# Low parts of the weight tiles: VectorE subtractions replaced by accumulating DMAs in SBUF, four weight buffers instead of three

## The chip, the cores and the metric

The kernel runs on one core of one Trainium2 chip. The metric is the device time of one execution in microseconds (us), as the median of several runs of the same kernel. Engines carry the names that the profile uses: PE is TensorE's matmuls and PEld its weight loads, DVE is VectorE, ACT is ScalarE, POOL is GpSimd, SP is SyncE, whose queue issues most DMAs.

## What is computed

Two identical layers of a hybrid decoder trunk over 512 positions and a model width of 1024, all inputs float32. Cut to what matters:

```python
h = rms_norm(x, ln_mix)
z = h @ w_in                                  # 1024 -> 6440 columns, split into the branches
o_nsa = nsa_attention(...)                    # compressed, selected and window attention, 8 heads
o_gla = gated_linear_attention(...)           # 4 heads, chunked
o_mem = memory_attention(...)                 # cross-attention into 256 memory tokens
merged = sum(gates[b] * (o_b @ w_branch[b]))  # three branches, 512 -> 1024 each
x = x + merged @ w_out
h = rms_norm(x, ln_mlp)
x = x + square(relu(h @ w_up)) @ w_down       # 1024 -> 4096 -> 1024
```

## The kernel before, in words

All large products are made in float32 quality from the faster `float32r` type. Each operand is split in two: a high part, which is the value rounded to `float32r`, and a low part, which is the value minus its high part. `mm3` (line 459) then makes three matmuls for one product: high by high, high by low and low by high. The activations are split once by `split` (line 492, high part on ACT, low part on DVE). The weights stream in: 128x1024 tiles of 512 KB, 298 whole ones and two more that come in halves at the start, 150 a layer.

`weights` (line 447) brings one tile in and takes three buffers from rings of three: `raw` for the loaded values, `wh` for the high part, `wl` for the low part. A load is issued on SP's queue, ACT casts `raw` to `wh`, and `self.low()` (line 360) names the engine that subtracts `wh` from `raw` into `wl`: DVE, except in the sparse-attention stage, where `share` is 4 and each fourth one goes to POOL. `raw` is free for the next load when both readers are done; `wh` and `wl` are free when the last matmul that reads them is done. `blockT` (line 604) uses a tile for 24 matmuls of 512 columns, `chunkM` (line 643) for 24 or 48 of 256 columns, `nsa_cmp` (line 1141) for 8 of 256 columns. `gate_proj` (line 841) takes one `raw` and one `wh` buffer from the same rings, for a small matrix whose two parts lie in one tile; it is made by ACT and DVE and stays so.

`layer` (line 1514) runs the stages of a layer: norm and compression keys, key and value projections, the compression MLP (`nsa_cmp`) woven with query and GLA projections, sparse attention woven with more projections, gated linear attention (GLA, `gla_attn`) woven with the first branch and the second gate, memory attention, the third branch, output projection, and the MLP, whose 64 tiles a layer serve 24 matmuls of 512 columns each.

The order of the instructions on each engine isn't the order of the code. `Order` (line 131) records every call with a cost from its table `time` (line 145), its tile dependencies and the rings' reuse, and `schedule` (line 234) lists the whole program on a time line of its own: `lat` gives the waiting time from one instruction to the next by the first one's engine. The order found is then forced on every engine's queue by dependencies. Since all calls go through one recording helper, nearly every instruction in the profile has line 312; rows are told apart by their tiles.

The names in the profile: `ps_d`, `ps_s`, `ps_t`, `ps_o` are PSUM banks; `xg` the split and scaled layer input, `u` the split hidden activations of the MLP or the merged branches; `nP`, `nd`, `nkraw`, `nqraw` belong to sparse attention; `ge`, `gke`, `gqz`, `gqe`, `gat`, `gS`, `grsa`, `grsy` to GLA; `xscr` is the scratch in HBM that carries `x` from the first layer to the second.

Of the kernel before, what the change touches and what calls it, by code (L numbers as in the profile page):

```python
# [9 lines left out]
F32 = mybir.dt.float32  # L10
F32R = mybir.dt.float32r
I32 = mybir.dt.int32
U8 = mybir.dt.uint8
AF = mybir.ActivationFunctionType
OP = mybir.AluOpType
# [4 lines left out]
P = 128  # L20
# [3 lines left out]
KT = D // P  # L24
# [106 lines left out]
class Order:  # L131
# [4 lines left out]
    def __init__(self, tc):  # L136
        self.tc = tc
        self.ins, self.eng, self.cost, self.pre = [], [], [], []
        self.load = []
        self.hist = {}  # L140
        self.first, self.ring, self.uses = {}, [], {}
        self.gone = []

    @staticmethod
    def time(eng, op, out, ins, accum):
# [27 lines left out]
    def note(self, eng, op, args, kw, r):  # L173
        is_ap = lambda x: hasattr(x, "tensor") and hasattr(x, "free_size")
        out = kw["out"] if "out" in kw else args[0]
        ins = [x for x in list(args[0 if "out" in kw else 1 :]) + [v for k, v in kw.items() if k not in ("out", "accum_out")] if is_ap(x)]
        outs = [out] + ([kw["accum_out"]] if "accum_out" in kw else [])
        k = len(self.ins)
        self.ins.append(r.ins)
        self.eng.append(eng)  # L180

        self.load.append(0.0 if eng != "tensor" else ins[0].free_size() / (2400 if op == "transpose" else 1200))
        self.cost.append(self.time(eng, op, out, ins, len(outs) > 1 and eng == "scalar"))
        pre = set()
        for w, aps in ((False, ins), (True, outs)):
            for x in aps:
                n = x.tensor.name
                h = self.hist.setdefault(n, [])
                if w and n in self.first:
                    f, prev, heads, m = self.first[n]  # L190
                    pre.update(f)
                    if prev:
                        self.ring.append((prev, k))
                    heads[m].append(k)
                    if m and heads[m - 1]:
                        pre.add(heads[m - 1][0])
                self.uses.setdefault(n, set()).add(k)
                a, b, c, d = g = self.region(x)
                keep = []
                for e in h:  # L200
                    (a2, b2, c2, d2), w2, k2 = e
                    if a < b2 and a2 < b and c < d2 and c2 < d:
                        if (w or w2 or x.space == PSUM) and k2 != k:
                            pre.add(k2)
                        if (w or x.space == PSUM) and k2 != k and a <= a2 and b2 <= b and c <= c2 and d2 <= d:
                            continue
                    keep.append(e)
                keep.append((g, w, k))
                self.hist[n] = keep
        self.pre.append(pre)  # L210
# [23 lines left out]
    def schedule(self):  # L234

        after = [[] for _ in self.pre]
        for k, p in enumerate(self.pre):
            for q in p:
                after[q].append(k)

        wait = {"sync": (2.0, 2.0), "tensor": (0.2, 0.0), "vector": (0.13, 0.25), "scalar": (0.14, 0.27), "gpsimd": (0.1, 0.1), "none": (0.0, 0.0)}

        def lat(a, b):
            return wait[self.eng[a]][self.eng[b] == "tensor"]


        start, end = self.go(self.pre, after, range(len(after)), lat, COLD)
        best = end, start
        for _ in range(3):
            back, end = self.go(after, self.pre, [-s - c for s, c in zip(start, self.cost)], lambda a, b: lat(b, a), 0.0)  # L250
            start, end = self.go(self.pre, after, [end - s - c for s, c in zip(back, self.cost)], lat, COLD)
            best = min(best, (end, start))
        self.start = best[1]
        info = mybir.DependencyInfo(mybir.DependencyClass.NoSync, mybir.DependencyReason.DATA)
        lines = {}
        for k in sorted(range(len(self.ins)), key=lambda k: self.start[k]):
            lines.setdefault(str(self.ins[k].engine), []).append(k)
        for o in lines.values():
            for a, b in zip(o, o[1:]):
                self.tc.add_manual_dep(self.ins[b], self.ins[a].name, info, reason="order")  # L260
# [91 lines left out]
class Builder:  # L352
# [93 lines left out]

    def weights(self, src, n=1024, parts=1):
        nc = self.nc
        raw = self.wp.tile([P, 1024], F32, name="raw", tag="raw", bufs=3)
        h = self.wp.tile([P, 1024], F32R, name="wh", tag="wh", bufs=3)  # L450
        l = self.wp.tile([P, 1024], F32R, name="wl", tag="wl", bufs=3)
        for p in range(parts):
            c = slice(p * n // parts, (p + 1) * n // parts)
            nc.sync.dma_start(raw[:, c], src[:, c])
            nc.scalar.copy(h[:, c], raw[:, c])
            self.low().tensor_sub(l[:, c], raw[:, c], h[:, c])
        return h, l

    def mm3(self, out, ops, start=True, stop=True):
# [381 lines left out]
    def gate_proj(self):  # L841

        nc = self.nc
        w = self.wp.tile([P, 1024], F32R, name="wh", tag="wh", bufs=3).rearrange("p (k x m) -> p k x m", k=KT, x=2)
        raw = self.wp.tile([P, 1024], F32, name="raw", tag="raw", bufs=3)[:, :512]
        nc.sync.dma_start(raw, self.a["ws"][self.l])
        r = raw.rearrange("p (k m) -> p k m", k=KT)
        nc.scalar.copy(w[:, :, 0], r)
        nc.vector.tensor_sub(w[:, :, 1], r, w[:, :, 0])
        ps = self.pd()  # L850

        for x, (h, l) in enumerate(self.xs()):
            both = w[:, x].rearrange("p x m -> p (x m)")
            self.nc.tensor.matmul(ps, both, h, start=x == 0, stop=False)
            self.nc.tensor.matmul(ps, both, l, start=False, stop=x == KT - 1)
            yield 0.43
        self.todo.append(lambda: self.gate_evac(ps))
# [827 lines left out]
```

## Time and profile before

| | |
|---|---|
| median of 3 runs | 1844.39 us (1839.19 to 1845.24) |
| the profiled execution | 1839.11 us, span 1837.3 us |
| granted clock of TensorE, mean over the span | 0.999 |
| moved by DMA | 174.03 MB, mean 95 GB/s |

The span runs from the first to the last instruction of the program on the profiled core; the 1.8 us more in the execution's own time lie around it. An engine's busy time is the time in which at least one of its instructions runs. A PE row's duration is longer than the distance to the next row, since matmuls are pipelined and their ends are modelled: the distance between starts is what a matmul costs.

### The profile page before, as it was taken

The page shows a single profiled execution, that of the slowest core. Times are in us where ns is not written, and L with a number is a line of the kernel's source. Part 1 is how long each engine was busy: PE and PEld are TensorE (multiplying, and loading weights), DVE is VectorE, ACT ScalarE, POOL GpSimd, SP SyncE. Part 2 cuts the span into 40 slices and gives each one's busy share as a digit, 9 for nine tenths or more (in the row PEclk, how much of TensorE's full clock was granted, in tenths as well). Part 3 has the DMA queues.
Part 4 walks back from the last instruction along what each step waited for, and adds up shares of the span by engine and source line. Part 5 has one row for each costly group of instructions (what it writes and reads, how often), then busy time and mean ns, then how long its engine had stood idle before and what let it go on. Part 6 is the DMA issues. An engine that isn't in the chain of part 4 may idle for free.

```text
span 1837.3 us, 26071 instructions
## 1 busy us (share of the span) xinstructions
PE 1809.5 (98%) x9832; PEld 1544.9 (84%) x9832; DVE 1118.4 (61%) x2373; ACT 809.3 (44%) x1642; POOL 271.7 (15%) x388
## 2 busy tenths in 40 slices
PE   8999999999999999999999999999999999999999
PEld 7988877898888888888899898779988888888888
DVE  8779979677554532343367889885874644324432
ACT  4547774455333421343334577643543334213321
POOL 1531125011001000001206311340010110000000
PEclk9999999999999999999999999999999999999999
DMA  5430121232242232323324211113323323232331
GB/s 179 135 114 24 47 70 56 94 127 93 93 137 92 93 102 92 104 92 114 115 98 140 68 35 59 58 62 101 126 80 98 132 93 103 92 104 92 100 113 63
DMA packets 50625, 174.03 MB, mean 95 GB/s; under 512 B 5922, under 2 KB 6340, under 8 KB 50244
## 3 DMA queue, kind: packets, MB, share of 16 engines
q1 hardware_dynamic: 49860, 170.28, 28.3%
q0 software_dynamic: 640, 2.10, 0.3%
q8 instruction: 77, 1.26, 0.3%
q14 instruction: 48, 0.39, 0.1%
HBM read 168.16 MB, written 4.19 MB: 94 GB/s over the span
## 4 chain that ended last, share of the span: by engine, by line
PE 89%; DVE 6%; POOL 2%; issue 1%; ACT 1%; DMA 0%; SPq 0%; DVEq 0%; ACTq 0%; POOLq 0%
PE ps_d L312 74%; PE ps_s L312 8%; PE ps_t L312 4%; PE ps_o L312 4%; DVE wl L312 1%; DVE gke L312 1%; POOL gqz L312 1%; DVE t L312 0%; POOL nkraw L312 0%; DVE nP L312 0%; ACT wh L312 0%; DVE ge L312 0%; DVE gat L312 0%; DVE grsa L312 0%; POOL t L312 0%
## 5 line engine op out<-in xcount | busy, mean ns | idle before, releaser
L312 ACT CAST wh<-raw 128x1024 fp32r<-128x1024 f32 (+1 forms) x304 | 316.7, 1045 | 636.7 <-PE ps_d L312 500.1
L312 PE MATMUL ps_d<-xg,wh 128*128 128x512 f32 x1888 | 596.5, 394 | 0.0
L312 DVE TENSOR_TENSOR wl<-raw,wh 128x1024 fp32r<-128x1024 f32 (+1 forms) x295 | 368.0, 1250 | 203.4 <-ACT wh L312 201.9
L312 PEld LDWEIGHTS ps_d<-xg,wh 128*128 128x128 f32 x1888 | 349.2, 188 | 68.7 <-issue 1.4
L312 PE MATMUL ps_d<-u,wh 128*128 128x512 f32 (+1 forms) x1248 | 376.2, 384 | 0.0
L312 PE MATMUL ps_d<-xg,wl 128*128 128x512 f32 x928 | 363.6, 392 | 0.4 <-DVE wl L312 0.4
L312 PEld LDWEIGHTS ps_d<-u,wh 128*128 128x128 f32 x1248 | 232.3, 188 | 46.1
L312 PE MATMUL ps_d<-wh,xg 128*128 128x256 f32 x1280 | 251.2, 286 | 0.0
L312 PE MATMUL ps_d<-u,wl 128*128 128x512 f32 (+1 forms) x624 | 239.3, 384 | 0.0
L312 PEld LDWEIGHTS ps_d<-wh,xg 128*128 128x128 f32 x1280 | 206.6, 192 | 2.9 <-issue 0.5
L312 PEld LDWEIGHTS ps_d<-xg,wl 128*128 128x128 f32 x928 | 174.3, 188 | 36.2 <-DVE wl L312 0.8
L312 PE MATMUL ps_d<-wl,xg 128*128 128x256 f32 x640 | 182.9, 286 | 0.6 <-DVE wl L312 0.6
L312 PEld LDWEIGHTS ps_d<-u,wl 128*128 128x128 f32 x624 | 117.3, 188 | 23.1
L312 DVE SCALAR_TENSOR_TENSOR t<-ps_d,rb 128x512 f32<-128x512 f32 x60 | 41.5, 691 | 144.1 <-PE ps_d L312 144.1
L312 PEld LDWEIGHTS ps_d<-wl,xg 128*128 128x128 f32 x640 | 122.7, 192 | 2.8 <-DVE wl L312 0.8
L312 DVE TENSOR_TENSOR x<-x,ps_d 128x512 f32<-128x512 f32 (+1 forms) x45 | 30.4, 676 | 140.8 <-PE ps_d L312 140.6
L312 ACT ACTIVATE nP<-nP,nm 128x32 f32<-128x32 f32 (+4 forms) x192 | 90.5, 475 | 13.4 <-DVE nm L312 13.1
L312 PE MATMUL ps_d<-oh,wh 128*128 128x512 f32 x192 | 77.1, 402 | 0.8 <-ACT oh L312 0.8
L312 DVE CUSTOM_DVE_ANT_0 nP<-ps_s,cst 128x32 f32<-128x32 f32 (+4 forms) x192 | 69.0, 384 | 13.4 <-PE ps_s L312 11.8
L312 PE MATMUL ps_d<-oh,wl 128*128 128x512 f32 x192 | 75.6, 394 | 0.0
L312 PE MATMUL ps_d<-ol,wh 128*128 128x512 f32 x192 | 75.2, 392 | 0.0
L312 POOL TENSOR_TENSOR accss<-accss,t 128x512 f32<-128x512 f32 x24 | 41.8, 1741 | 219.6 <-ACT t L312 132.6
(311 smaller groups left out, 2515.7 us busy)
## 6 DMA issues: line engine op xcount, KB each, us to landing
raw<-wu SPq DMA_DIRECT2D x64, 512.0 KB, 3.5
raw<-wd SPq DMA_DIRECT2D x64, 512.0 KB, 3.5
raw<-wt SPq DMA_DIRECT2D x58, 512.0 KB, 3.5
raw<-wm SPq DMA_DIRECT2D x40, 512.0 KB, 3.5
raw<-wb SPq DMA_DIRECT2D x24, 512.0 KB, 3.5
raw<-wc SPq DMA_DIRECT2D x16, 512.0 KB, 3.5
raw<-wkv SPq DMA_DIRECT2D x16, 512.0 KB, 3.4
raw<-wo SPq DMA_DIRECT2D x16, 512.0 KB, 3.5
```

Of the source, the lines that this page charges most:

```text
L312: r = f(*args, **kw)
```

## The change

`weights` no longer subtracts. For a whole tile, ACT writes a second copy, the high part times -1, into `wl`, and a DMA issued from POOL's queue adds the 512 KB of `raw` onto it in SBUF (`accum_op=OP.add`), so that `wl` holds raw minus high as before. The two tiles that come in halves (`parts` > 1) keep the DVE subtraction. The rings of `raw`, `wh` and `wl` have four buffers. The scheduler counts 4.0 us from the issue of any DMA on POOL's queue to its reader (before 0.1 us, as for any POOL instruction). The room for the three further buffers of 4 KB a partition comes from the space for descriptors of POOL's DMAs, which is set to 4096 bytes a partition. `low()`, `share` and `turn` stay in the code, but no one calls `low()` any more.

```diff
@@ Order
+        self.far = set()
...
+        if eng == "gpsimd" and op == "dma_start":
+            self.far.add(k)
...
         def lat(a, b):
-            return wait[self.eng[a]][self.eng[b] == "tensor"]
+            return 4.0 if a in self.far else wait[self.eng[a]][self.eng[b] == "tensor"]
@@ Builder.weights
-        raw = self.wp.tile([P, 1024], F32, name="raw", tag="raw", bufs=3)
-        h = self.wp.tile([P, 1024], F32R, name="wh", tag="wh", bufs=3)
-        l = self.wp.tile([P, 1024], F32R, name="wl", tag="wl", bufs=3)
+        raw = self.wp.tile([P, 1024], F32, name="raw", tag="raw", bufs=4)
+        h = self.wp.tile([P, 1024], F32R, name="wh", tag="wh", bufs=4)
+        l = self.wp.tile([P, 1024], F32R, name="wl", tag="wl", bufs=4)
         for p in range(parts):
             c = slice(p * n // parts, (p + 1) * n // parts)
             nc.sync.dma_start(raw[:, c], src[:, c])
             nc.scalar.copy(h[:, c], raw[:, c])
-            self.low().tensor_sub(l[:, c], raw[:, c], h[:, c])
+            if parts > 1:
+                nc.vector.tensor_sub(l[:, c], raw[:, c], h[:, c])
+                continue
+
+            nc.scalar.activation(l[:, c], h[:, c], AF.Copy, scale=-1.0)
+            nc.gpsimd.dma_start(l[:, c], raw[:, c], accum_op=OP.add)
@@ Builder.gate_proj
-        w = self.wp.tile([P, 1024], F32R, name="wh", tag="wh", bufs=3).rearrange("p (k x m) -> p k x m", k=KT, x=2)
-        raw = self.wp.tile([P, 1024], F32, name="raw", tag="raw", bufs=3)[:, :512]
+        w = self.wp.tile([P, 1024], F32R, name="wh", tag="wh", bufs=4).rearrange("p (k x m) -> p k x m", k=KT, x=2)
+        raw = self.wp.tile([P, 1024], F32, name="raw", tag="raw", bufs=4)[:, :512]
@@ kernel
-    nc = bacc.Bacc("TRN2", target_bir_lowering=False, num_devices=1)
+    nc = bacc.Bacc("TRN2", target_bir_lowering=False, num_devices=1, dynamic_dma_scratch_size=4096)
```

The scheduler turns this into other queues. Three places are shown.

DVE in GLA of the first layer, around the product that scales the first chunk's output (`t` from `ps_o` and `grsy`). Before:

```order
L312 TENSOR_TENSOR t_3621<-ps_o,grsy 128x512
L312 SCALAR_TENSOR_TENSOR acc<-th,ps_d 128x512
L312 TENSOR_TENSOR wl<-raw,wh 128x1024
L312 COPY_PREDICATED gat<-lvl,ps_s 128x2x128
L312 TENSOR_TENSOR gke<-gkT,ge 128x256
L312 COPY_PREDICATED gat<-lvl,ps_s 128x2x128
L312 TENSOR_TENSOR wl<-raw,wh 128x1024
L312 TENSOR_TENSOR ge<-bT 128x256
```

Changed:

```order
L315 TENSOR_TENSOR t_3658<-ps_o,grsy 128x512
L315 SCALAR_TENSOR_TENSOR acc<-th,ps_d 128x512
L315 COPY_PREDICATED gat<-lvl,ps_s 128x2x128
L315 TENSOR_TENSOR gke<-gkT,ge 128x256
L315 COPY_PREDICATED gat<-lvl,ps_s 128x2x128
L315 TENSOR_TENSOR ge<-bT 128x256
```

Two subtractions of weight tiles are gone from between the instructions of GLA, and nothing stands in their place.

POOL at the same place of GLA, from the products that fill `gqz` for the next chunk. Before:

```order
L312 TENSOR_TENSOR gqz_3387<-gqT,ge 64x2x64 x2
L312 TENSOR_TENSOR gqz_3389<-gqT,ge 64x2x64 x2
L312 TENSOR_TENSOR gqz_3391<-gqT,ge 64x2x64 x2
L312 TENSOR_TENSOR t_3621<-t_3621,rn 128x512
L312 TENSOR_TENSOR gqz_3387<-gqT,ge 64x2x64 x2
L312 TENSOR_TENSOR gqe<-gqe,gqT 128x256
L312 MEMSET gat 128x512
L312 TENSOR_TENSOR gqz_3389<-gqT,ge 64x2x64 x2
```

Changed:

```order
L315 TENSOR_TENSOR gqz_3422<-gqT,ge 64x2x64 x2
L315 TENSOR_TENSOR gqz_3424<-gqT,ge 64x2x64 x2
L315 TENSOR_TENSOR gqz_3426<-gqT,ge 64x2x64 x2
L315 TENSOR_TENSOR t_3658<-t_3658,rn 128x512
L315 DMA wl<-raw 128x1024
L315 TENSOR_TENSOR gqe<-gqe,gqT 128x256
L315 DMA wl<-raw 128x1024
L315 TENSOR_TENSOR gqz_3422<-gqT,ge 64x2x64 x2
L315 MEMSET gat 128x512
L315 TENSOR_TENSOR gqz_3424<-gqT,ge 64x2x64 x2
L315 DMA wl<-raw 128x1024
L315 TENSOR_TENSOR gqz_3422<-gqT,ge 64x2x64 x2
```

Three issues of accumulating DMAs now stand between POOL's own products; each waits for ACT's negated copy, and what stands behind it waits with it.

ACT in the first layer where `nsa_cmp` is woven with the query projection (`nkT` and `nkl` are the turned and split keys). Before:

```order
L312 COPY nkT_496<-ps_t_586 128x4x128
L312 CAST wh_1004<-raw_1003 128x1024
L312 CAST nkl_606<-nkraw_338 128x4x128
L312 CAST wh_1019<-raw_1018 128x1024
L312 COPY nkT_496<-ps_t_630 128x4x128
L312 CAST wh_1077<-raw_1076 128x1024
```

Changed:

```order
L315 COPY nkT_498<-ps_t_583 128x4x128
L315 ACTIVATE wl_944<-wh_943 128x1024
L315 CAST wh_967<-raw_966 128x1024
L315 COPY nkT_498<-ps_t_589 128x4x128
L315 ACTIVATE wl_968<-wh_967 128x1024
L315 CAST nkl_609<-nkraw_338 128x4x128
L315 COPY nqraw_238<-ps_d_748 128x256
```

Each cast of a weight tile has now a second ACT instruction of the same size behind it, which reads the cast's result.

## Rows read from the trace of the kernel before

**Rows 1.** Page, part 1: busy time, share of the span and instructions of each engine.
```profile
PE 1809.5 (98%) x9832; PEld 1544.9 (84%) x9832; DVE 1118.4 (61%) x2373; ACT 809.3 (44%) x1642; POOL 271.7 (15%) x388
```
**Rows 2.** Timeline of PE in the first layer's MLP: start us, duration us, instruction.
```profile
699.70 0.39 PE L312 MATMUL ps_d<-u,wl 128*128 128x512 f32 x1
699.93 0.62 PE L312 MATMUL ps_d<-u,wh 128*128 128x512 f32 x2
700.38 0.39 PE L312 MATMUL ps_d<-u,wl 128*128 128x512 f32 x1
```
**Rows 3.** Busy time by stage: window, length, engines (count), clock, DMA share, GB/s.
```profile
138.00:276.00 138.00, 135.94 (x853) 117.06 (x852) 121.82 (x403) 104.83 (x289) 25.71 (x48) 1.00 0.14 47
276.00:322.00 46.00, 43.41 (x240) 33.43 (x239) 42.19 (x102) 19.21 (x61) 25.90 (x38) 1.00 0.18 58
...
460.00:920.00 460.00, 460.00 (x2042) 381.18 (x2041) 199.73 (x240) 156.35 (x203) 28.66 (x21) 1.00 0.32 103
...
1012.00:1150.00 138.00, 134.41 (x921) 119.86 (x920) 120.39 (x401) 95.85 (x267) 29.79 (x51) 1.00 0.16 51
1150.00:1242.00 92.00, 88.07 (x473) 69.11 (x471) 77.49 (x191) 49.12 (x133) 35.57 (x56) 1.00 0.19 64
```
**Rows 4.** Groups of instructions on weight tiles: DVE and ACT (page), POOL (by shape).
```profile
L312 ACT CAST wh<-raw 128x1024 fp32r<-128x1024 f32 (+1 forms) x304 | 316.7, 1045 | 636.7 <-PE ps_d L312 500.1
L312 DVE TENSOR_TENSOR wl<-raw,wh 128x1024 fp32r<-128x1024 f32 (+1 forms) x295 | 368.0, 1250 | 203.4 <-ACT wh L312 201.9
L312 POOL TENSOR_TENSOR wl<-raw,wh 128x1024 fp32r<-128x1024 f32 x7 | 16.7, 2385 | 54.2 <-ACT wh L312 31.4 <-DVE nd L312 22.9
```
**Rows 5.** Chain that ended last, both GLA stretches, pieces of weight tiles: start, us.
```profile
279.71 1.35 DVE wl L312
...
298.73 2.01 DVE wl L312
301.66 1.21 DVE wl L312
...
1192.14 1.34 DVE wl L312
...
1211.15 2.28 DVE wl L312
1214.35 1.21 DVE wl L312
```
**Rows 6.** Groups on DVE from 138 to 276 us, by shape: two of them.
```profile
L312 DVE TENSOR_TENSOR wl<-raw,wh 128x1024 fp32r<-128x1024 f32 x10 | 12.1, 1216 | 0.1
...
L312 DVE TENSOR_SCALAR nP<-nP,nd 128x512 f32<-128x512 f32 x12 | 5.5, 484 | 0.0
```
**Rows 7.** DMA issues by tile: queue, count, size, median us from issue to landing.
```profile
raw<-wd SPq DMA_DIRECT2D x64, 512.0 KB, 3.5
...
xscr<-x POOLq DMA_DIRECT2D x8, 256.0 KB, 2.3
```
**Rows 8.** POOL's instructions on xscr: duration of an issue, ns min/median/max.
```profile
L312 POOL DMA_DIRECT2D xscr<-x x8: 545/557/748, 847.3 to 923.5; - x8
```
**Rows 9.** SP's DMA queue from 640 to 680 us: packets, MB, share of sixteen engines.
```profile
q1 hardware_dynamic: 1008, 3.67, 28.1%
```
**Rows 10.** ACT's casts in four stretches: 60:100, 360:400, 980:1020 and 1280:1320 us.
```profile
L312 ACT CAST wh<-raw 128x1024 fp32r<-128x1024 f32 x12 | 12.7, 1057 | 7.6 <-PE ps_d L312 7.5
...
L312 ACT CAST wh<-raw 128x1024 fp32r<-128x1024 f32 x10 | 10.5, 1046 | 5.1 <-PE ps_d L312 3.0 <-issue 2.1
...
L312 ACT CAST wh<-raw 128x1024 fp32r<-128x1024 f32 x12 | 12.6, 1056 | 7.8 <-PE ps_d L312 4.5 <-PE ps_s L312 3.3
...
L312 ACT CAST wh<-raw 128x1024 fp32r<-128x1024 f32 x11 | 11.5, 1046 | 6.4 <-PE ps_d L312 3.7 <-issue 2.1 <-ACT t L312 0.5
```
**Rows 11.** POOL's products for GLA's queries, over the whole span.
```profile
L312 POOL TENSOR_TENSOR gqz<-gqT,ge 64x128 f32<-64x128 f32 x64 | 36.0, 563 | 29.7 <-PE ps_s L312 16.0 <-ACT ge L312 11.0
```

## The prediction

> **What bounds the kernel now.** I read the page's busy times first. PE is busy 1809.5 of 1837.3 us, DVE 61%, ACT 44%, POOL 15% [rows 1]. The change takes no matmul away, so at most the 27.8 us in which PE shows idle can be won, and a little that hides: in a dense stretch a matmul starts every 0.227 us (three take 0.68) while its row shows 0.39 [rows 2], so a pause of up to 0.16 us after each leaves no idle time in the page. The table by stage tells where the idle time lies. In the MLP, PE is busy 460.0 of 460.0 us and DVE 199.7 [rows 3]: nothing is to be had there. In sparse attention PE is idle 138.0 - 135.9 = 2.1 us in the first layer and 138.0 - 134.4 = 3.6 in the second, in GLA 46.0 - 43.4 = 2.6 and 92.0 - 88.1 = 3.9 [rows 3]. In these four, DVE is busy 84 to 92% and is the fullest engine after PE. The chain that ended last agrees: outside them it is nearly all PE, and in GLA it runs for tens of us from one DVE instruction to the next, six subtractions of weight tiles among them [rows 5].
>
> **The change, part by part.** The sum is made against the profiled execution of 1839.1 us; the median of the runs is 1844.4, 5.3 more, and that is added at the end.
>
> DVE loses 295 instructions less the four halves that stay, some 364 us of 1250 ns each [rows 4]; POOL loses seven of 2385 ns. Where DVE isn't late this is worth nothing. In GLA it is: the six pieces on the chain last 1.35 + 2.01 + 1.21 + 1.34 + 2.28 + 1.21 = 9.4 us [rows 5], and the order of DVE shows their places empty. What is late next is the rest of the same DVE chain, and POOL's products beside it. The gain can't be over what PE loses there, 6.5 us shown [rows 3] and the pauses that hide: ends 0 and -12, and I take **-8**, a little under the pieces' sum. In sparse attention ten subtractions of 1216 ns go from DVE [rows 6], but PE loses only 2.1 and 3.6 us [rows 3]: ends 0 and -6, taken **-4**.
>
> ACT gains 298 copies of the size of its cast, 1045 ns [rows 4]: 311 us, which brings it from 809 to 1120 of 1837. The fullest stage is sparse attention, where ten copies take it from 104.8 to some 115 of 138 us [rows 3]; cost 0, covered by ACT's idle time, and 10 if that cover fails where a softmax row stands behind a copy.
>
> POOL gains 298 issues. The nearest row is its own issue of the scratch store, 557 ns [rows 8]: 166 us, so that it ends at some 420 of 1837. The price of the wait in front of each is in a rival below.
>
> The way from a free buffer to a low part gets longer. Before it was cast and subtraction, 1.05 + 1.25 = 2.3 us [rows 4]. Now it is cast, copy, issue and landing. A landing of an accumulating DMA isn't in the trace: a store of 256 KB from POOL takes 2.3 us, a load of 512 KB 3.5 [rows 7]; the DMA must read two sources, so the other end is twice 3.5, 7.0. I take 5.1, the load and one more pass of 1.6 (next paragraph). The sum is 1.05 + 1.05 + 0.56 + 5.1 = 7.8 us. Cover: with four buffers a tile's buffers come free three tiles ahead of its use. In the MLP a tile lasts 24 x 0.227 = 5.45 us [rows 2], so 16.3 us; in the stretches with most tiles a tile comes every 3.3 us [rows 10], so 10. Cost 0. At 7.0 the way is 9.7 us and still fits, barely, where two woven stages don't hold a buffer longer.
>
> The DMA engines get a second transfer for each tile. From 640 to 680 us, SP's queue moved 3.67 MB, seven tiles, in 28.1% of the time of sixteen engines [rows 9]: 11.2 us, 1.6 a tile. The accumulating DMA takes the same if it is limited by what it writes, and 3.2 if by its two reads; no row is nearer to either end, so I take the middle, 2.4, and 4.0 for a tile in all. In the MLP 4.0 of 5.45 us are used, and nothing waits. In four stretches of 40 us, 12, 10, 12 and 11 tiles are cast [rows 10]; they need 48, 40, 48 and 44 us, so 8, 0, 8 and 4 are missing. The tiles that stand ready at the start of a stretch pay back 4 us each: with one, 4 + 0 + 4 + 0 = 8 us stay, with two, nothing. I take **+4**.
>
> The start: the two tiles in halves stay with DVE, and the order of the matmuls is the old one over the first 40 us of PE's work. Cost 0, -2 to +4. The smaller space for descriptors costs nothing unless more DMAs are in flight than fit; four buffers hold at most four.
>
> Sum: -8 - 4 + 4 = **-8**: 1831 for a profiled execution, **1836** on the scale of the median.
>
> **The rivals.** *The DMA engines can't keep up (slower).* The mechanism is that of the paragraph above with 3.2 us for the accumulating DMA: 4.8 for a tile, 57.6, 48, 57.6 and 52.8 us in the four stretches, 56 too much in all, less one tile's 4.8 in each: +37 where the sum has +4. -8 - 4 + 37 = +25: **1869**. It decides from where the shortage passes the gain of 12: 45 tiles times c, less 160 us, less 4c, is 12 at c = 4.2, so from 2.6 us for the accumulating DMA on. For it speaks that the DMA reads two tiles to write one; against it, that both lie in SBUF, while the row's 1.6 us are for reads from HBM. The Trainium skill (DMA: Bandwidth & Descriptors, Issuing engines are not separate DMA queues) says that transfers from all queues run on the same engines and interleave, so that a second queue brings no bandwidth. By it the two times add up, as this rival and the sum have them; if POOL's queue were free of SP's, the +4 would go and the time be 1832. No row of before has both queues full at once.
>
> *POOL's queue holds up GLA.* POOL is busy 25.9 of 46 us in GLA [rows 3], and its products of 563 ns [rows 11] are on the chain. Six issues a layer now stand between them, and each waits for ACT's copy. Where POOL arrives early, it stands for up to 1.05 us and then issues for 0.56: 12 x 1.6 = 19 us on the chain that loses 9.4. With no gain in attention either and the same +4 dropped, that is +10: **1854**. It decides from 9.4 / 12 = 0.8 us an issue. Against it speaks that the order puts the copies well before. A rule stands beside it, in the Trainium skill (SBUF — State Buffer, the "DVE blocks DMA" trap): while DVE runs an operation that takes the port pair it shares with GpSimd, GpSimd can't write descriptors. By that rule an issue is late by up to one such operation; the likely kind here, of 484 ns [rows 6], times 12 would add 6 us and give 1860. The store's issues, 545 to 748 ns [rows 8], show no such wait, but DVE was lightly loaded there.
>
> *Nothing moves.* PE is the bound, the idle time in GLA passes from the subtractions to the rest of the chain, and the small costs eat what is left: **1844**.
>
> *The MLP becomes DMA-bound.* From 5.45 - 1.6 = 3.85 us for the accumulating DMA on, every tile waits. With three passes, two reads and a write one after the other, it takes 4.8: 6.4 - 5.45 = 0.95 us for some 168 tiles of the MLP and the stages like it (918 us by 5.45), +160, and the four stretches on top: about **2030**. For it speaks nothing but that the price isn't in the trace.
>
> **How the numbers follow.** A measurement of this kernel can tell 0.3%, 5.5 us, from no change. Chances: the forecast 0.5, with a range of its own from 1824 to 1845 by its ends; DMA engines short 0.2; POOL's queue 0.1; nothing 0.13; the MLP bound by DMA 0.07. Of the forecast 0.08 lies within 5.5 us of the old time, so faster 0.42, the same 0.08 + 0.13 = 0.21, slower 0.2 + 0.1 + 0.07 = 0.37. The range begins at 1822, where GLA and attention both give their full ends and the stretches cost nothing (-18, and -4 for pauses that hide elsewhere). Above, it takes in POOL's rival and most of the first one: 1875. Left out are the last rival and the far part of the first.
>
> **What would show it.** Right: DVE near 755 us busy, ACT near 1120, POOL's issues near 0.6 us and landing within some 5, PE's idle time in the two GLA windows down by half, and the MLP still at 460 of 460. The first rival shows as PE idle in the four stretches of 40 us, ended by a DMA onto `wl`, with the DMA share near 1 there. The second shows as POOL idle in GLA ended by ACT's `wl`, with `gqz` late behind it. The last shows as PE idle throughout the MLP. The forecast is wrong if an accumulating DMA keeps the sixteen engines for over 2.6 us, or if the chain in GLA is as long as before without the six pieces.

## The result and the profile after

The changed kernel takes 1857.15 us in the median of 4 runs (1853.17 to 1860.82), the kernel before 1842.76 beside it: a ratio of 1.0079, with a 95% interval from 1.0051 to 1.0108. It is **slower by 0.8%**. The forecast was 1836, faster; the time lies inside the range, between the forecast and the first rival's 1869, and the profile shows that rival at work: the DMA engines can't keep up.

The page of the changed kernel, the profiled execution of 1853.17 us: busy times, DMA queues (packets, MB, share of sixteen engines), engines of the chain that ended last, the two new groups of instructions, and DMA issues.

```profile
PE 1812.2 (98%) x9832; PEld 1544.0 (83%) x9832; DVE 768.9 (42%) x2082; ACT 1090.3 (59%) x1940; POOL 473.8 (26%) x679
...
q0 software_dynamic: 43552, 158.35, 45.4%
q1 hardware_dynamic: 49860, 170.28, 28.9%
...
PE 86%; DMA 6%; DVE 3%; ACT 2%; issue 1%; POOL 1%; SPq 0%; POOLq 0%; ACTq 0%; DVEq 0%
...
L315 POOL DMA_DIRECT2D wl<-raw x298 | 259.2, 870 | 1062.2 <-ACT wl L315 938.0
...
L315 ACT ACTIVATE wl<-wh 128x1024 fp32r<-128x1024 f32 x298 | 314.0, 1054 | 3.5
...
wl<-raw POOLq DMA_DIRECT2D x298, 512.0 KB, 5.6
raw<-wu SPq DMA_DIRECT2D x64, 512.0 KB, 4.8
raw<-wd SPq DMA_DIRECT2D x64, 512.0 KB, 4.7
```

DVE is relieved as the change says, from 1118.4 to 768.9 us, and PE is busy for as long as before to within 2.7 us [rows 1]. What is new stands in the lines on DMA. POOL's queue holds the sixteen engines for 45.4% of 1851.4 us. Without its 0.3% of other transfers, the share that it has in the runs without adding DMAs, that is 835 us for 298 tiles: **2.80 us a tile**. A load holds them for 0.289 x 1851.4 / 325 = 1.65 us (170.28 MB are 325 tiles). Loads of 512 KB land after 4.8 us where they took 3.5 [rows 7].

PE's waits name the same thing: engine, tile, what it waited for, us in total, times, longest.

```profile
PE ps_d L315 <- DMA wl<-raw: 20.4, 21, 2.5
PE ps_s L315 <- ACT wh L315: 7.4, 1, 7.4
PE ps_s L315 <- DMA wl<-raw: 1.4, 2, 1.0
```

The second line is the start of the kernel and is as long in the kernel before. The other two, 21.8 us, are new; from 60 to 120 us they are 8.9 us of the 9.3 that PE shows idle there. Where they stand is shown by the table by stage, with windows moved by what the kernel is late there (columns as in [rows 3]: window, length, busy PE, PEld, DVE, ACT, POOL, clock, DMA share, GB/s):

```profile
144.00:282.00 138.00, 136.93 (x862) 118.03 (x861) 107.86 (x391) 117.51 (x299) 29.52 (x55) 1.00 0.39 91
282.00:325.50 43.50, 42.34 (x241) 33.93 (x240) 36.11 (x97) 24.19 (x67) 30.26 (x47) 1.00 0.56 137
465.00:925.00 460.00, 460.00 (x2045) 381.28 (x2044) 103.20 (x163) 233.73 (x287) 95.69 (x106) 1.00 0.85 198
1027.00:1161.00 134.00, 134.00 (x914) 119.49 (x913) 103.58 (x386) 106.38 (x279) 24.34 (x45) 1.00 0.46 111
1161.00:1251.00 90.00, 87.91 (x479) 70.23 (x478) 63.99 (x184) 59.95 (x144) 42.77 (x69) 1.00 0.53 129
```

In sparse attention PE is now idle for 1.1 and 0 us, where it was 2.1 and 3.6, in GLA 1.2 and 2.1, where it was 2.6 and 3.9 [rows 3]. The MLP is full as before. So the gain is there, and the loss lies outside these five windows, in the stretches with most tiles: the compression stage `nsa_cmp` (60 to 120 us, again from 980) and the projections for the memory (from 380 and from 1300). Before:

```profile
60.00:80.00 20.00, 18.76 (x157) 18.28 (x157) 15.27 (x32) 11.32 (x18) 12.06 (x21) 1.00 0.47 142
80.00:100.00 20.00, 19.57 (x126) 17.42 (x125) 14.26 (x31) 10.72 (x17) 8.33 (x13) 1.00 0.56 177
100.00:120.00 20.00, 19.97 (x124) 17.00 (x123) 14.23 (x36) 4.97 (x7) 17.09 (x35) 1.00 0.35 126
380.00:400.00 20.00, 19.41 (x162) 19.17 (x161) 18.87 (x58) 13.11 (x38) 6.60 (x7) 1.00 0.52 175
1000.00:1020.00 20.00, 18.02 (x91) 14.56 (x90) 16.29 (x31) 7.49 (x10) 14.58 (x27) 1.00 0.45 143
```

Changed:

```profile
60.00:80.00 20.00, 16.96 (x143) 16.41 (x141) 7.68 (x25) 14.24 (x22) 8.73 (x13) 1.00 1.02 240
80.00:100.00 20.00, 16.56 (x110) 14.67 (x109) 8.18 (x25) 12.42 (x17) 11.68 (x20) 1.00 1.05 259
100.00:120.00 20.00, 17.13 (x85) 13.16 (x84) 5.01 (x9) 10.93 (x13) 13.35 (x37) 1.00 1.00 253
380.00:400.00 20.00, 17.77 (x145) 17.16 (x144) 9.56 (x30) 14.68 (x39) 9.62 (x12) 1.00 1.01 238
1000.00:1020.00 20.00, 16.85 (x96) 14.56 (x95) 8.68 (x24) 11.83 (x17) 12.30 (x25) 0.91 1.02 252
1300.00:1320.00 20.00, 17.61 (x141) 16.80 (x139) 5.16 (x29) 13.61 (x33) 4.21 (x5) 1.00 0.95 232
```

PE is idle for 2.2 to 3.4 us of each 20, where it was 0 to 2.0. The DMA share, which was 0.35 to 0.56, is 0.95 to 1.05. The share is the sum of the packets' times over that of sixteen engines; that it passes 1 means that packets overlap, and that the engines have no time left. DMA queues and issues from 60 to 120 us (below), where before one queue took 45.6%:

```profile
q0 software_dynamic: 2096, 7.60, 67.3%
q1 hardware_dynamic: 2218, 7.38, 34.5%
...
wl<-raw POOLq DMA_DIRECT2D x15, 512.0 KB, 7.2
raw<-wm SPq DMA_DIRECT2D x6, 512.0 KB, 7.0
```

7.60 MB are 14.5 tiles, so 0.673 x 60 / 14.5 = 2.79 us for an adding DMA, and 7.38 MB are 14.1, so 1.47 for a load: 4.26 us a tile. In 60 us fourteen tiles have room; before, twelve were cast in 40 [rows 10]. The chain through the same stretch spends 30.8 of the 48.9 us from 59.75 to 108.63 in four landings (start, us, what); between them stand work of ACT, DVE and POOL and 5.3 us of PE:

```profile
59.75 6.26 DMA wl<-raw
...
66.06 7.65 DMA raw<-wc
...
83.17 7.45 DMA wl<-raw
...
99.23 9.40 DMA wl<-raw
```

How the difference grows can be read by counting: how much later than in the kernel before the k-th matmul starts, in the profiled executions. (The order of the matmuls differs inside woven stages, so the numbers are read at the ends of stages.) The columns after the first are the changed kernel and the runs of the next section. They hold the granted clock too: its mean over the profiled execution is 0.999 before, in the change, e3 and b1, but 0.994 in e1, 0.989 in e6, 0.987 in e5 and 0.991 in e8. (1 - clock) times the span, an estimate as if PE were busy throughout, is 1.8 us before, 11 in e1, 21 in e6, 25 in e5 and 17 in e8.

```
 k    before  after   e1    e2    e3    e4    e5    e6    e8    b1    b2
 400    69.3   -1.3  +3.9  +3.8  -1.3  -0.7  +7.2  -0.0  +5.0  -0.5  -1.9
 700   115.6   +7.8  +7.7  +3.9  -0.5  +1.6 +24.8 +15.5 +17.2  +2.3  +7.0
2000   328.0   +3.3  +8.9  +1.7  -5.2  -2.9 +19.9 +15.9 +16.0  -0.1  +3.0
2800   451.8   +8.6  +9.0  +1.8  -5.4  +1.3 +34.6 +22.6 +18.6  -0.5  +5.4
5300   980.9   +6.0  +8.9  +1.8  -8.3  +2.4 +40.7 +21.0 +19.3  -1.9  +3.0
5500  1008.6  +14.8  +9.8  +2.7  -5.3  +7.0 +56.9 +31.7 +24.5  +4.3  +9.8
7200  1286.2   +8.8 +12.2  -2.6 -10.3  +2.8 +50.7 +37.0 +19.3  -0.6  +3.7
7600  1345.0  +14.1 +12.3  -2.5 -10.1  +2.8 +66.2 +41.2 +23.3  -0.6  +4.8
9800  1830.0  +14.1 +12.3  -2.5 -10.2  +2.8 +73.5 +41.2 +23.3  -0.6  +4.8
```

The changed kernel loses 9.1 us in the compression stage of the first layer (400 to 700), 5.3 in the memory's projections (2000 to 2800), 8.8 in the second layer's compression (5300 to 5500) and 5.3 in its memory (7200 to 7600): 28.5. It gains 4.5 in attention and GLA of the first layer, 6.0 in those of the second, 1.3 at the start and 2.6 ahead of the second compression stage: 14.4. The sum is +14.1.

### The profile page after: what moved, and what is told of

The parts are those of the page before. It is cut to its first block, busy times and chain, and to the rows that moved or that the text cites. A ratio compares the mean times of both kernels' runs of the same rounds, so it can differ in the third digit from the quotient of the medians.

```text
span 1851.4 us, 26737 instructions
## 1 busy us (share of the span) xinstructions
PE 1812.2 (98%) x9832; PEld 1544.0 (83%) x9832; DVE 768.9 (42%) x2082; ACT 1090.3 (59%) x1940; POOL 473.8 (26%) x679
## 3 DMA queue, kind: packets, MB, share of 16 engines
q0 software_dynamic: 43552, 158.35, 45.4%
q1 hardware_dynamic: 49860, 170.28, 28.9%
## 4 chain that ended last, share of the span: by engine, by line
PE 86%; DMA 6%; DVE 3%; ACT 2%; issue 1%; POOL 1%; SPq 0%; POOLq 0%; ACTq 0%; DVEq 0%
PE ps_d L315 71%; PE ps_s L315 7%; PE ps_t L315 4%; DMA wl<-raw 4%; PE ps_o L315 4%; DMA raw<-wb 1%; DMA raw<-wc 1%; DVE ge L315 0%; ACT wl L315 0%; ACT wh L315 0%; DVE gke L315 0%; DMA raw<-wt 0%; DVE xg L315 0%; POOL gqz L315 0%; POOL nkraw L315 0%
## 5 line engine op out<-in xcount | busy, mean ns | idle before, releaser
L315 POOL DMA_DIRECT2D wl<-raw x298 | 259.2, 870 | 1062.2 <-ACT wl L315 938.0
L315 ACT ACTIVATE wl<-wh 128x1024 fp32r<-128x1024 f32 x298 | 314.0, 1054 | 3.5
L315 DVE TENSOR_TENSOR u<-t,u 128x512 fp32r<-128x512 f32 x64 | 44.1, 692 | 120.5 <-ACT u L315 120.5
```

Of the source, the lines that this page charges most:

```text
L315: r = f(*args, **kw)
```

## The experiments

Two theories stand against each other. **A**: the sixteen DMA engines are full where tiles come fastest, because an adding DMA holds them for 2.8 us. **B**: it is the way from a free buffer to its low part, 1.05 us cast, 1.05 negation, 0.87 issue and 5.6 landing, 8.6 in all, that is too long for four buffers. All times are medians, beside 16 or 17 runs of the kernel before on the same chip (1843.21 us for e1, e2, e3 and e6, 1842.4 for e4, e5 and b1, 1839.16 for e8 and b2), with the 95% interval of the ratio in brackets.

### e1: four buffers, subtraction on DVE and POOL

```diff
-            if parts > 1:
-                nc.vector.tensor_sub(l[:, c], raw[:, c], h[:, c])
-                continue
-
-            nc.scalar.activation(l[:, c], h[:, c], AF.Copy, scale=-1.0)
-            nc.gpsimd.dma_start(l[:, c], raw[:, c], accum_op=OP.add)
+            self.low().tensor_sub(l[:, c], raw[:, c], h[:, c])
...
-            return 4.0 if a in self.far else wait[self.eng[a]][self.eng[b] == "tensor"]
+            return wait[self.eng[a]][self.eng[b] == "tensor"]
```

> Four buffers as in the change, but the low parts made by VectorE and GpSimd as before (and the scheduler's latencies as before). It tells what the fourth buffer alone does. Theory A (the sixteen DMA engines are full where tiles come fastest: 2.8 us for an accumulating DMA and 1.5 for a load, 4.3 for a tile that is wanted every 3.3 to 4; some +29 us in four stretches, some -14.5 from the relieved VectorE elsewhere): 1843, within 1838 to 1847, since neither the load on the DMA engines nor that on VectorE differs from before. Theory B (the way from a free buffer to the low part, 1.05 + 1.05 + 0.87 + 5.6 = 8.6 us, is too long for four buffers; the engines themselves would do): 1843 as well. If the -14.5 were the fourth buffer's and not VectorE's, 1829.

Measured 1848.61 us, 1.0034 [1.0022, 1.0046]: a miss. A fourth buffer, with the order that the scheduler finds for it, is 5 us worse. The loss stands in the first 700 matmuls and in the second layer's attention (table), with the DMA engines as lightly loaded as before (29.3% and 0.3%). PE's waits of this run show where the new order is softer: PE waits 5.2 us for the split keys of sparse attention, 1.4 before, and 2.4 for a turned tile, 2.0 before:

```profile
PE ps_t L315 <- ACT nkl L315: 5.2, 2, 2.9
PE ps_t L315 <- DVE t L315: 2.4, 1, 2.4
```

The clock may have a part in the 5 us: the six executions were granted 0.994 or 0.995, those before mostly 0.997 to 0.999. What follows: buffers and order are a part of the change of their own, and what the adding DMA costs has to be read from runs of the same order.

### e3: the same order, a plain copy in place of the adding DMA

```diff
-            nc.gpsimd.dma_start(l[:, c], raw[:, c], accum_op=OP.add)
+            nc.gpsimd.dma_start(l[:, c], raw[:, c].bitcast(F32R))
```

> The changed kernel in the same order of all instructions, but the DMA copies raw onto the low part and adds nothing, so the subtraction is left out. Theory A: a copy reads one source in place of two, so it keeps the engines some 1.3 to 1.6 us and not 2.8, a tile takes about 3 us, and the four stretches lose next to nothing: 1830, within 1826 to 1838, DMA share in the stretches near 0.75 in place of 1.0. Theory B: the way is shorter by the difference of the landings alone, some 1.3 of 8.6 us, and more than half of the loss stays: 1843 to 1852.

The DMA leaves the addition out: `wl` is overwritten with `raw`. Measured 1829.25 us, 0.9929 [0.9916, 0.9941]: 14 us faster than before, as theory A has it. Every engine's order is that of the change, row by row, so the 28 us between the medians of this run and the change come from the DMA and what it brings about; at the same granted clock, 0.999 in both profiled executions, it is 24.2 (spans of 1851.4 and 1827.2). Page of this run (DMA queue, POOL's group, landing) and the first two windows:

```profile
q0 software_dynamic: 43552, 158.35, 23.9%
...
L315 POOL DMA_DIRECT2D wl<-raw x298 | 162.9, 546 | 1118.7 <-ACT wl L315 984.7
...
wl<-raw POOLq DMA_DIRECT2D x298, 512.0 KB, 3.5
```

```profile
60.00:80.00 20.00, 18.97 (x163) 18.82 (x162) 8.04 (x25) 15.85 (x24) 9.43 (x19) 1.00 0.84 278
80.00:100.00 20.00, 19.29 (x116) 16.36 (x115) 8.29 (x25) 14.04 (x21) 10.87 (x25) 1.00 0.91 311
```

The same bytes by a copy hold the engines for 0.236 x 1827.2 / 298 = **1.45 us**, half as long as the addition, and the share in the stretch falls from 1.02 and 1.05 to 0.84 and 0.91. The four stretches lose 0.8, -0.2, 3.0 and 0.2 us, 3.8 instead of 28.5 (table). But the copy also lands earlier, 3.5 us against 5.6, and issues faster, 0.55 against 0.87, so this run alone doesn't part A from B.

### e6: the kernel before, with adding DMAs whose sums nobody reads

```diff
+        self.dump = [self.wp.tile([P, 1024], F32R, name=f"dump{i}") for i in range(2)]
...
             self.low().tensor_sub(l[:, c], raw[:, c], h[:, c])
+            if parts == 1:
+                self.dumped += 1
+                nc.gpsimd.dma_start(self.dump[self.dumped % 2], h, accum_op=OP.add)
```

> The kernel before (three buffers, VectorE subtraction) with one more accumulating DMA a tile, which adds the high part onto one of two tiles that nobody reads; nothing is left out of the computation. PE never waits for this DMA and the low part comes by the short way. Theory A: the engines are as full as in the change, the loads come late in the four stretches: 20 to 30 us more than before, 1863 to 1873. Theory B: no low part is late, 1843 to 1847.

Measured 1877.93 us, 1.0189 [1.0173, 1.0206]: 35 us slower, more than A expected. No low part comes from a DMA here, so a late low part isn't needed for a loss. The queue's line and a window of the first stretch:

```profile
q0 software_dynamic: 43552, 158.35, 49.7%
```

```profile
80.00:100.00 20.00, 16.84 (x106) 14.83 (x105) 12.25 (x21) 7.79 (x13) 11.18 (x16) 0.91 1.05 273
```

The share is 1.05 as in the change, and the loss stands in the same four stretches (+15.5, +6.7, +10.7, +4.2 in the table). It is larger than the change's: there are three buffers here, DVE keeps its subtractions, and PE waits for DVE's `wl` (10.9 us) and `t` (8.8 us), where it waited for them 1.9 and 2.0 us before. But the run doesn't part A from B cleanly, since its DMAs are waited for after all:

```profile
POOL dump L312 <- DMA dump<-wh: 336.9, 84, 5.4
ACT wh L312 <- DMA dump<-wh: 26.4, 13, 3.3
```

ACT's next cast waits until a DMA has read `wh`, and POOL, with its own products behind it, until the DMA before has landed on the same one of the two tiles. By the estimate above, some 19 us of the loss can be the lower clock.

### e5: the change with three buffers

```diff
-        raw = self.wp.tile([P, 1024], F32, name="raw", tag="raw", bufs=4)
-        h = self.wp.tile([P, 1024], F32R, name="wh", tag="wh", bufs=4)
-        l = self.wp.tile([P, 1024], F32R, name="wl", tag="wl", bufs=4)
+        raw = self.wp.tile([P, 1024], F32, name="raw", tag="raw", bufs=3)
+        h = self.wp.tile([P, 1024], F32R, name="wh", tag="wh", bufs=3)
+        l = self.wp.tile([P, 1024], F32R, name="wl", tag="wl", bufs=3)
...
```

> The change with three weight buffers as before, the adding DMA kept. Theory A: the engines' work is the same, only the credit of one ready tile (about 4 us at each of four places at most) is gone: 1857 to 1870 us. Theory B: the way of 8.6 us has one buffer less to run beside, and PE waits for low parts at most tiles of the fast stretches and in the MLP: above 1880.

Measured 1914.68 us, 1.04 [1.0384, 1.0416]: as theory B expected, and A's 1857 to 1870 is missed by far. Windows of this run:

```profile
60.00:80.00 20.00, 16.13 (x124) 15.50 (x122) 5.73 (x12) 12.89 (x20) 12.32 (x28) 0.91 0.90 210
80.00:100.00 20.00, 16.01 (x128) 15.15 (x128) 8.71 (x32) 13.10 (x20) 10.57 (x17) 1.00 0.90 205
100.00:120.00 20.00, 15.30 (x53) 12.42 (x54) 4.93 (x12) 7.25 (x7) 13.66 (x36) 0.74 0.91 205
```

PE loses more than in the change, and the DMA engines are no longer full: 0.90 against 1.02. With three buffers the way is the bound, since two tiles ahead cover 2 x 3.3 = 6.6 us [rows 10] of a way of 8.6. In the MLP, where two tiles last 10.9 us, only 6 us are lost (2800 to 5300 in the table). So B names a true bound, and the fourth buffer lifts it where the engines have room: in the change, the same DMAs land after 4.5 us in the median from 144 to 282 us, where the share is 0.39, so the way is 7.5 us and under the 10 us of cover; from 60 to 120 us, at a share of 1.02, they land after 7.2 us, and the way of 10.2 us just passes it. With four buffers it is the full engines that make the way too long.

There is a second round that neither theory counted. `raw` now comes free only when the adding DMA has landed, so SP's queue, which issues the loads, waits in the change from 60 to 125 us for

```profile
SPq L315 <- DMA wl<-raw: 62.1, 16, 6.7
```

A `raw` buffer goes through load, cast, copy, issue and landing: with light DMA 3.5 + 1.05 + 1.05 + 0.87 + 4.5 = 11.0 us (an estimate from the durations above), 2.7 us a tile with four buffers and 3.7 with three. A tile is wanted every 3.3. e3 has the same wait (61.8 us) and loses nothing by it, so with four buffers it is no bound of its own.

### e8: plain copies, and a second copy that nobody reads

```diff
...
             nc.gpsimd.dma_start(l[:, c], raw[:, c].bitcast(F32R))
+            self.dumped += 1
+            nc.gpsimd.dma_start(self.a["dump"][self.dumped], h[:, c])
```

> The run with plain copies in place of the adding DMAs (1829 us), with a second copy of each weight tile's high part, from SBUF to a DRAM buffer that nobody reads, issued on GpSimd right behind the first; the subtraction is left out as there. The low part is there as early as with one copy unless the engines are full; the engines' work is about 1.45 + 1.45 + 1.6 = 4.5 us a tile, as in the change (2.8 + 1.5 = 4.3). Theory A (the sixteen DMA engines are full where tiles come fastest): the loss of the change in the stretches of cmp and memory comes back: 1857 us (1848 to 1870). Theory B (with four buffers it is the adding DMA's own long way): 1829 to 1838, with a little for the second issue on GpSimd.

Measured 1859.8 us, 1.011 [1.0097, 1.0123]: A's 1857 within its range, B's 1829 to 1838 missed. Queue, landing and two windows:

```profile
q0 software_dynamic: 86464, 314.61, 46.7%
...
wl<-raw POOLq DMA_DIRECT2D x298, 512.0 KB, 4.1
```

```profile
400.00:420.00 20.00, 17.84 (x136) 16.86 (x136) 10.54 (x47) 14.47 (x37) 6.93 (x12) 1.00 1.05 360
1000.00:1020.00 20.00, 19.75 (x148) 19.18 (x148) 9.46 (x26) 13.30 (x21) 12.65 (x27) 0.84 0.95 327
```

Two copies hold the engines for 0.464 x 1860.6 / 298 = 2.90 us, as the one addition does (2.80), while the landing is 4.1 us and the issue 0.55: the way is 1.05 + 1.05 + 0.55 + 4.1 = 6.8 us instead of 8.6, and yet the time is the change's. The first stretch loses more here (+17.2 by matmul 700) than in the change. The second issue on POOL and the longer hold of `wh` stand in that too: from 60 to 125 us ACT's casts wait 7.9 us for the second copy to have read `wh`, and the share there is 0.86 to 0.96, not 1. In the four stretches the run loses 24.0 us, and ahead of them 5; by the estimate above, some 15 us of all that can be the lower clock. So a second transfer without any addition makes the loss come back, but that its size agrees so well is luck.

### e2: the adding DMA only in attention and GLA

```diff
-            if parts > 1:
+            if parts > 1 or not self.acc:
                 nc.vector.tensor_sub(l[:, c], raw[:, c], h[:, c])
                 continue
```

`acc` is set from the attention stage's start to the end of GLA, in each layer. 52 of the 298 tiles stay with the adding DMA.

> Accumulating DMAs in the sparse attention and GLA stages alone, VectorE subtractions everywhere else, four buffers. Theory A: the four stretches of many tiles lose nothing, PE gains the 4.6 and 6.0 us that it gained between them in the change: 1832, within 1828 to 1837, faster than both kernels. Theory B: 1832 too, if the way is short enough where tiles come slowly. If the loss had come from GpSimd's queue in attention and GLA: above 1845.

Measured 1839.33 us, 0.9977 [0.9968, 0.9986]: faster, but 7 us short of what was expected. The table says why: the first 700 matmuls lose 3.9 with DVE alone, nearly all of it in the first 400, where e1 has lost as much (the wait for `nkl` is the same 5.2 us), and attention and GLA then give back 2.2 and 5.3. The run shows that the adding DMA gains in these two stages whatever is done elsewhere; in the change they hold 10.5 of the 14.4 us gained. There is also a window in which the engines are full and PE loses nothing; why it doesn't was not looked into:

```profile
100.00:120.00 20.00, 20.00 (x116) 16.87 (x114) 11.06 (x31) 11.31 (x14) 12.72 (x28) 1.00 1.02 237
```

So a share of 1 over 20 us doesn't by itself cost time. The price of an adding DMA is (0.081 - 0.003) x 1834.8 / 52 = 2.75 us here, where the engines are seldom full: the 2.80 isn't made by crowding.

### e4: half of each tile by the adding DMA, half by DVE

```diff
-            nc.scalar.activation(l[:, c], h[:, c], AF.Copy, scale=-1.0)
-            nc.gpsimd.dma_start(l[:, c], raw[:, c], accum_op=OP.add)
+            d = slice(0, n // 2)
+            e = slice(n // 2, n)
+            nc.scalar.activation(l[:, d], h[:, d], AF.Copy, scale=-1.0)
+            nc.gpsimd.dma_start(l[:, d], raw[:, d], accum_op=OP.add)
+            nc.vector.tensor_sub(l[:, e], raw[:, e], h[:, e])
```

> The change, but only half of each low tile's columns is made by the adding DMA; VectorE subtracts the other half; four buffers. Theory A (the sixteen DMA engines are full where tiles come fastest): an adding DMA holds the engines about 1.4 us instead of 2.8, with the load's 1.6 some 3.0 a tile instead of 4.3, so the two stretches of cmp and memory lose little and VectorE is relieved of half its subtraction: 1836 us (1831 to 1841), faster than before. Theory B (the way from a free buffer to its low part is too long for four buffers): cast, negation and issue are as long as in the change and only part of the landing is shorter, so the stretches go on losing: about 1850 (1846 to 1856).

Measured 1837.82 us, 0.9974 [0.9961, 0.9987]: A's 1836 holds. Half a tile takes (0.240 - 0.003) x 1840.1 / 298 = 1.46 us of the engines, so the price goes with the bytes. The compression stage of the first layer now loses 2.3 us (matmul 400 to 700) instead of 9.1, and the four stretches 11.1 instead of 28.5, in the slowest of the twelve executions. POOL issues as many DMAs as in the change and each takes as long (298, 875 ns in the mean), so the issues aren't what costs the change its time. The half also lands after 3.5 us, so B has a share in this one.

### b1 and b2: DVE for the tiles of the full stretches

```diff
-            if parts > 1:
+            if parts > 1 or dve:
                 nc.vector.tensor_sub(l[:, c], raw[:, c], h[:, c])
                 continue
...
-                w = self.weights(a["wc"][l, kind, c])
+                w = self.weights(a["wc"][l, kind, c], dve=True)
```

The key and value weights of the memory get the same through an argument of `chunkM`; 16 tiles a layer in all.

> The change, but the 16 tiles a layer of the compression weights and of the memory's key and value weights are made by VectorE's subtraction; all others by the adding DMA; four buffers. Theory A: in the two stretches that lost 28.6 us in all, a good part of the tiles asks 1.6 us of the DMA engines instead of 4.3, so most of the loss goes and the gains of 14.5 us in attention and in the gated scan stay: 1832 us (1828 to 1838), faster than both kernels. Theory B: the tiles beside them are as late as ever, and the loss stays: 1845 or more. The run of four buffers with VectorE lost 6 us in the first stretch by the new order alone; if that loss comes back here, 1838 to 1842.

Measured 1833.9 us, 0.9962 [0.9947, 0.9977]: faster than both kernels, 8.5 us under the one before. Windows of this run:

```profile
60.00:80.00 20.00, 18.91 (x164) 18.71 (x163) 13.34 (x28) 13.54 (x22) 9.42 (x17) 1.00 0.73 198
80.00:100.00 20.00, 18.45 (x115) 16.16 (x114) 13.37 (x30) 13.39 (x19) 10.41 (x17) 1.00 0.81 220
100.00:120.00 20.00, 19.40 (x109) 15.62 (x107) 12.21 (x36) 9.57 (x14) 13.79 (x37) 1.00 1.00 241
```

With the share at 0.73 and 0.81, and at 1 only in the last 20 us, the first stretch loses 2.8 us (400 to 700) and the memory's projections lose nothing in either layer, although most tiles beside those 16 take the same long way (landing 5.6 us in the page, 6.2 from 60 to 120). The second compression stage still loses 6.2. The table is of an execution of 1838.81, the slowest of the six, so its end of -0.6 is less than the median's gain.

b2 gives half the columns of the 16 tiles back to the adding DMA:

```diff
...
-            if parts > 1 or dve:
+            if parts > 1:
                 nc.vector.tensor_sub(l[:, c], raw[:, c], h[:, c])
                 continue
+
+            if dve:
+                e = slice(n // 2, n)
+                c = slice(0, n // 2)
+                nc.vector.tensor_sub(l[:, e], raw[:, e], h[:, e])
...
```

> As the version with VectorE's subtraction for the 16 tiles a layer of the compression and the memory weights (1834 us), but half the columns of those 16 tiles by the adding DMA. Theory A: they ask 3.0 us of the DMA engines instead of 1.6; if the stretches are full even so, 1836 to 1842; if not, VectorE is relieved of half of their subtraction and it is 1830 to 1835. Theory B: 1840 or more, since the landing of the half tile is late in the same places.

Measured 1841.13 us, 1.0007 [0.9993, 1.0021], so no gain is left. It falls in A's branch of 1836 to 1842, though the share, 0.92, 0.89 and 1.02 from 60 to 120 us, is not at 1 throughout; the first stretch loses 8.9, with the granted clock at 0.93 to 0.97 in it. B expected 1840 or more as well, so this run doesn't tell the two apart. Sixteen half tiles a layer decide over the 0.45% by which b1's ratio is ahead.

## Why the prediction was wrong

**The step that failed** is the term of the DMA engines, "so I take the middle, 2.4, and 4.0 for a tile in all ... I take +4". An adding DMA holds the engines for 2.80 us, halfway from the middle to the end of two reads, 3.2; a plain copy of the same bytes takes 1.45 (e3), so the addition doubles it. Counted in such copies the two ends that the prediction put at 1.6 and 3.2, from loads out of HBM, are 1.45 and 2.90: the measured price is not in the middle but close to that of two reads. By the prediction's own rule for the first rival, with 1.6 + 2.8 = 4.4 us, 45 x 4.4 - 160 - 4 x 4.4 = 20 us, less the gain of 12, is +8: 1853 on the median's scale. Its point of decision, 2.6 us, was passed. The measured 1857 lies between this and the rival's 1869.

**The credit of ready tiles** was over-counted too. With the 4.26 us a tile measured from 60 to 120 us, the four stretches of 12, 10, 12 and 11 tiles lack 11.1, 2.6, 11.1 and 6.9 us, 31.7 together; the stretches lost 28.5. Hardly one tile's credit was paid in all, where the term counted one or two in each stretch. The stretches are also longer than the 40 us that were counted: the share stood at 1 from 60 to 120 us. Which of the two it was, no run tells.

**What held.** The gains were of the right size in the sum, 10.5 us in attention and GLA where -8 and -4 were taken. The same order with a cheap copy ends 10.1 us early in the profiled execution (span 1827.2 against 1837.3), and 14 in the median. GLA alone gives less than -8 and attention a little more than -4: by the same count of matmuls, at the ends of the windows of [rows 3], the change goes from +5.9 to +3.3 in the first layer's GLA and from +11.8 to +8.8 in the second's, 5.6 us, and PE's shown idle time falls from 6.5 to 3.3. The MLP stays at 460.0 of 460.0 with a DMA share of 0.85 (4.0 of 5.45 us were forecast, 0.73), so the rival in which it becomes DMA-bound is out. ACT's copies are covered: 1054 ns each, ACT 1090 us busy, and none of PE's waits is for one of them.

**The other terms.** POOL's issue was taken at 0.56 us and is 0.87, over the 0.8 at which the second rival was to decide. It still didn't come true: PE waits for `gqz` four times for 1.4 us in all, and GLA is faster than before, so the 19 us of that rival aren't there. What the issues cost inside the chain of GLA wasn't measured. The landing was taken at 5.1 us and is 5.6, and 7.2 in the full stretch; the way is 8.6 us in the median where 7.8 was taken, under the 10 us of cover, and 10.2 in the full stretch, just over it. With one buffer less it was decisive (e5), so "cost 0" holds for four buffers with room on the DMA engines and no further. The last rival's 2030 is a slip in the sum: it took the first rival's 37 us for the four stretches, where its own 6.4 us a tile give 102, so some 2095; the rival is out either way.

POOL's issues last 844 ns at the least, 862 in the median and 1160 at the most in the changed kernel (its instructions on `wl`), and loads that go beside them land after 4.8 us instead of 3.5. The rule cited from the Trainium skill (DMA: Bandwidth & Descriptors, Issuing engines are not separate DMA queues), that transfers of all queues share the same engines, agrees: the shares of the two queues, 67.3% and 34.5%, add up to one full set. The other rule cited from the Trainium skill (SBUF — State Buffer, the "DVE blocks DMA" trap) shows no effect in these durations, whose maximum is 0.3 us over the least. Single issues are longer in other runs, 1592 ns in e4 and 1910 in e6, each beside an operation of DVE; whether that is the cause, or whether a descriptor is written late behind an issue's record, no run here shows.

**What stays open.** That the addition costs the 28 us is shown by e3. That it does so through the engines' time and not by the landing's length alone rests on the count (31.7 us lacking, 28.5 lost), on the landings of 4.5 and 7.2 us in one and the same kernel, and on e4 and b1; e6 and e8, made to part the two, have waits of their own. How much of e1's 5 us is the order, the clock or a hold of buffers wasn't tried: a run with four buffers in the old order would tell. The second compression stage of b1 still loses 6 us, and its cause wasn't looked for.

## What to carry to other kernels

Before work is moved from an engine to a DMA, the DMA engines' time is to be counted as an engine's time, by stretch and not by span: here 74% over the span was too much, because the tiles come in bursts and the four stretches stood at 0.95 to 1.05. An operation that no compute engine runs isn't free, and an adding DMA cost twice the copy of the same bytes. So give the DMA the tiles of the stages in which it is idle and the other engine is late, and leave the bursts to the engine: that version (b1) is faster than either of the two pure ones, by 8.5 us and by 23. A longer way from load to use needs its buffers counted against the fastest stretch, from the moment in which a buffer comes free to the next such moment.

## What the runs showed of the hardware

- A DMA of 512 KB within SBUF holds the sixteen engines for 1.45 us as a copy (e3) and 2.80 us as an addition (2.75 in e2, 2.83 in e5, 3.1 in e6). Half the columns cost half (1.46). It lands after 3.5 and 5.6 us, and its issue on POOL takes 530 and 862 ns in the median.
- The granted clock fell in some of the stretches in which PE paused, though not in all: 0.91 from 1000 to 1020 us in the changed kernel, 0.83 in e6 and 0.84 in e8 in the same window, 0.74 from 100 to 120 us in e5, but 1.00 from 60 to 120 us in the changed kernel, where PE was idle for 2.9 to 3.4 us of each 20. Of the two levels, 1.2 and 2.4 GHz, a mean of 0.91 means that about a fifth of the window was granted the lower one. In the lower one a matmul takes about twice as long: in e6, matmuls of 128x512 onto `ps_d` by `wl` last 389 ns in the median and at most 796, the longest at 92.0 us, where the clock is 0.91 over the window from 80 to 100. So a wait that a DMA causes can cost more than its own length. The four runs of the change spread by 7.7 us along with it: 0.999 over the execution of 1853.2 us, 0.994 over that of 1860.8.
